# Attention in one core's two-layer model: inverse sums transposed later, low parts of the output weights pinned in order

## The chip, the cores and the metric

The program runs on one core of a Trainium2 chip. TensorE (PE) multiplies, VectorE (DVE), ScalarE (ACT) and GpSimd (POOL) do the rest, SyncE (SP) issues most of the transfers. The metric is the device time of one execution in microseconds (us): 1930.66 for the kernel before, the median of 3 runs (1925.57 to 1931.99).

## The reference

Two layers on 512 tokens of width 1024, in float32, and a last normalisation. Each layer is a feed-forward stage (added at half weight), a mixer and a second feed-forward stage; the mixer of the first layer joins gated linear attention with softmax attention of 8 heads, that of the second lets 16 heads look at the best keys only.

```
for layer in range(2):
    x = x + 0.5 * swiglu(rmsnorm(x, g[0]), ffn_w_in[layer, 0], ffn_w_out[layer, 0])
    h = rmsnorm(x, g[1])
    x = x + (even_mixer(h) if layer % 2 == 0 else odd_mixer(h))
    x = x + 0.5 * swiglu(rmsnorm(x, g[2]), ffn_w_in[layer, 1], ffn_w_out[layer, 1])
return rmsnorm(x, final_norm_g)

even_mixer: concat(gla(h), softmax(q k / 8 + F_i - F_j) v) @ even_w_out     # causal, 8 heads of 64
odd_mixer:  score = sum_h w_h relu(q_idx_h k_idx)                # 8 heads, causal
            idx = top_k(score, 128)                              # per query
            p = softmax(q_lat c[idx] / 8 + t5_bias)              # 16 heads
            (p c[idx]) @ w_uv @ odd_w_out
```

## The kernel before, in words

Activations lie with features on the 128 partitions and the 512 tokens along the free dimension, in 8 tiles of 128x512. A float32 product is made of three products of rounded parts: weights and activations are each split into a high part (`whi`, rounded by ACT) and a low part (`wlo`, the rest, subtracted by DVE), and `mm3` (L195 to L200) multiplies high with high, high with low and low with high. `Weights.split` (L76 to L89) makes the two parts of 1024 columns of a load; it is called from `at` when a product first needs them, one piece ahead. There are 3 buffers each for high and low parts and 2 for the raw loads (`wraw`).

The stages follow each other: feed-forward 0, even mixer, feed-forward 1 and 2, odd mixer, feed-forward 3. In the odd mixer the search for the best keys (`topk`, from L1137) finds 8 maxima (`m8`) and strikes them out of the scores (`acc`), 16 times for each of three blocks of queries, on DVE. It is woven with the products of the queries.

`attention` (from L639) serves both mixers. Its work is a list of units, one for each pair of heads, block of 128 queries (`b`, 0 to 3) and head of the pair, so 8 units a pair; block `b` sees 128(b+1) keys. There are 4 pairs in the even mixer and 8 in the odd one. In step `i` of the main loop: the bias of unit i+2 is added up on POOL, the scores of unit i are multiplied on PE (bank `s`) and joined with the bias on DVE, which also finds the row's extreme (L665, tiles `p` and `l`); the probabilities of unit i-4 are transposed on PE (bank `pt`, L680) and copied out, by ACT or DVE in turn (L683, L685, tiles `pts`); ACT takes the exponential of unit i (L672) and sums it. Values (`values`, L688) of block `b` are multiplied six steps after its second unit into the bank `o`.

At the end of a pair DVE inverts the 8 columns of sums and spreads them (L724, L725, tile `r`); four transposes on PE bring them to the layout of `o` (L701), ACT copies them out (L703, `rb`); two steps after the last values of the pair DVE multiplies `o` by `rb` (L708, called the normalisation here), ACT rounds the result (L712), DVE takes its low part (L715).

PSUM has 2 banks for `ps`, 3 for `s`, 2 for `pt` and 1 for `o`. PE executes in the order in which the code is written (`manual_schedule`). On the other engines a scheduler orders the instructions by program position and its own estimate of when they are ready; `keep_in_program_order` takes an instruction out of that choice. All engines work off their own order one instruction after the other, and the tracker of tiles adds the waits.

`out_units` (from L541) is the output projection: 4 loads of 2048 columns, each for two tiles of the result, 8 groups of three products for a tile. Groups 0 to 6 of the first three tiles are mixed into the last 8 steps of the attention, two groups a step; the rest follows.

Of the kernel before, what the change touches and what calls it, by code (L numbers as in the profile page):

```python
# [8 lines left out]
F32 = mybir.dt.float32  # L9
# [8 lines left out]
KT = D // 128  # L18
# [12 lines left out]
NB = S // 128  # L31
# [10 lines left out]
class Filler:  # L42


    def __init__(self):
        self.q, self.done = [], set()
# [22 lines left out]
class Weights:  # L69


    def __init__(self, b, raw, n, piece, pool_lo):
        self.b, self.raw, self.n, self.piece, self.pool_lo = b, raw, n, piece, pool_lo
        self.parts = {}

    def split(self, j):  # L76
        b, nc = self.b, self.b.nc
        c = j * self.piece
        if c >= self.n or j in self.parts:
            return  # L80
        m = min(self.piece, self.n - c)
        hi, lo = b.wtile(m)
        x = self.raw[:, c:c + m]
        nc.scalar.activation(hi, x, AF.Copy)  # L84
        if self.pool_lo:
            nc.gpsimd.tensor_tensor(lo, x, hi.bitcast(F32), op=OP.subtract)
        else:
            nc.vector.tensor_sub(lo, x, hi.bitcast(F32))  # L88
        self.parts[j] = (hi, lo)  # L89

    def at(self, c, m):
# [72 lines left out]
class Builder:  # L164
# [34 lines left out]
        mm(ps, w[0], x[1], start=False, stop=False)  # L199
        mm(ps, w[1], x[0], start=False, stop=last)  # L200

    def load_w(self, src, n, pool_lo=False, piece=1024, cuts=()):
        raw = self.wraw.tile([128, n], F32, name="wraw")
        e = [0, *cuts, n]
        for a, b in zip(e[:-1], e[1:]):
            self.nc.sync.dma_start(raw[:, a:b], src[:, a:b])
        return Weights(self, raw, n, piece, pool_lo)

    def scaled(self, i, gcol):

# [330 lines left out]
    def out_units(self, src, O, after):  # L541

        nc = self.nc
        W, P = {}, {}

        def part(d, ks):
            for k in ks:
                self.mm3(P[d], W[d // 2].at((d % 2 * KT + k) * 128, 128), O[k], k == 0, k == KT - 1)

        def begin(d, tag):  # L550
            if d % 2 == 0:
                W[d // 2] = self.load_w(src[d // 2], 2 * KT * 128)
            P[d] = self.bank(tag)

        def end(d):
            with self.tc.high_priority(offset=60):
                nc.vector.tensor_add(self.X[:, d], P[d], self.X[:, d])
                after(d)

        early = 3  # L560
        for d in range(early):
            begin(d, "ps" if d < 2 else "pt")
            for k in range(KT - 1):
                part(d, [k])
                yield 0.65
        yield "last"
        self.next_in()
        for d in range(early):
            part(d, [KT - 1])
            end(d)  # L570
        for d in range(early, KT):
            begin(d, "ps")
            part(d, range(KT))
            end(d)
# [64 lines left out]
    def attention(self, n_pairs, setup, A, head, bias, fill, act_share, ahead):  # L639

        nc = self.nc
        units = [(pair, b, hh) for pair in range(n_pairs) for b in range(NB) for hh in range(2)]
        P, T, H, steps = {}, {}, {}, []

        def add_bias(i):
            pair, b, hh = units[i]  # L650
            P[units[i]] = bias(H[2 * pair + hh], 2 * pair + hh, b)

        def scores(pair, b, hh):
            a = A[pair]
            if "l" not in a:
                a["l"] = self.at.tile([128, 16], F32, name="l", bufs=3)
            n = 128 * (b + 1)
            s = self.bank("s")
            q, kh, kl = a["qk"]
            for k in (kh, kl):  # L660
                nc.tensor.matmul(s[:, :n], q[hh][:, b * 128:b * 128 + 128], k[hh][:, :n], start=k is kh, stop=k is kl)  # L661
            t = P[pair, b, hh]
            u = 2 * b + hh
            m = a["l"][:, 8 + u:9 + u]
            nc.vector.tensor_tensor_reduce(out=t[:, :n], in0=s[:, :n], in1=t[:, :n], scale=-1.0, scalar=3.0e38,  # L665
                                           op0=OP.add, op1=OP.min, accum_out=m)

        def exps(pair, b, hh):
            l = A[pair]["l"]
            u = 2 * b + hh  # L670
            t = P[pair, b, hh][:, :128 * (b + 1)]
            nc.scalar.activation(t, t, AF.Exp, bias=l[:, 8 + u:9 + u], scale=-1.0, accum_out=l[:, u:u + 1])  # L672

        def transpose(i):
            u = units[i]
            n = 128 * (u[1] + 1)
            pt = self.bank("pt")
            t = P.pop(u)
            for k in range(0, n, 128):
                nc.tensor.transpose(pt[:, k:k + 128], t[:, k:k + 128], self.ident)  # L680
            ts = self.at.tile([128, S], F32, name="pts", bufs=5)
            if i % 4 < act_share:
                nc.scalar.activation(ts[:, :n], pt[:, :n], AF.Copy)  # L683
            else:
                nc.vector.tensor_copy(ts[:, :n], pt[:, :n])  # L685
            T[u] = ts

        def values(i, pair, b):  # L688
            a = A[pair]
            if b == 0:  # L690
                a["o"] = self.bank("o")
            for kb in range(b + 1):
                for hh in range(2):
                    v = a["V"][kb][:, a["vcol"] + hh * 64:a["vcol"] + hh * 64 + 64]
                    nc.tensor.matmul(a["o"][hh * 64:hh * 64 + 64, b * 128:b * 128 + 128], v,  # L695
                                     T[pair, b, hh][:, kb * 128:kb * 128 + 128], start=kb == 0, stop=kb == b)
            if b == NB - 2:

                rb = self.bank("pt")
                for c in range(NB):  # L700
                    nc.tensor.transpose(rb[:, c * 128:c * 128 + 128], a["r"][:, c * 128:c * 128 + 128], self.ident)  # L701
                a["rb"] = self.at.tile([128, S], F32, name="pts", bufs=5)
                nc.scalar.activation(a["rb"], rb, AF.Copy)  # L703
            if b == NB - 1:
                o = []

                def norm():
                    nc.vector.tensor_mul(a["rb"], a["o"], a["rb"])  # L708

                def high():  # L710
                    o.append(a["dst"]())
                    nc.scalar.activation(o[0][0], a["rb"], AF.Copy)  # L712

                def low():
                    nc.vector.tensor_sub(o[0][1], a["rb"], o[0][0].bitcast(F32))  # L715

                for j, f in enumerate((norm, high, low)):
                    later.setdefault(i + 2 + j, []).append(f)

        def inverse(a):  # L720

            a["r"] = self.at.tile([128, S], F32, name="pts", bufs=5)
            l = a["l"][:, :8]
            nc.vector.reciprocal(l, l)  # L724
            nc.vector.tensor_copy(a["r"].rearrange("p (u d) -> p u d", d=64), l[:, :, None].to_broadcast([128, 8, 64]))  # L725

        def prepare(i):

            pair = units[i][0]
            for h in range(2 * pair, 2 * min(pair + 2, n_pairs)):  # L730
                if h not in H and (h < 2 or i % 8 > 3):
                    H[h] = head(h)
            for p in range(pair, min(pair + 1 + ahead, n_pairs)):
                if p not in A and (p == 0 or i % 8 > 0):
                    g = setup(p)
                    next(g)
                    steps.append(g)
            if steps:
                try:
                    next(steps[0])  # L740
                except StopIteration:
                    steps.pop(0)

        n = len(units)
        later = {}
        prepare(0)
        for i in range(BIAS_LEAD):
            add_bias(i)
        for i in range(n + LAG + 3):
            if i < n:  # L750
                prepare(i)
                if i + BIAS_LEAD < n:
                    add_bias(i + BIAS_LEAD)
                scores(*units[i])
            if 0 <= i - LAG < n:
                transpose(i - LAG)
            if i < n:
                exps(*units[i])
                if i % 8 == 7:
                    later.setdefault(i + 2, []).append(lambda a=A[units[i][0]]: inverse(a))  # L760
            for f in later.pop(i, ()):
                f()
            fill(i)
            j = i - LAG - 2
            if 0 <= j < n and units[j][2] == 1:
                values(i, *units[j][:2])
        for i in sorted(later):
            for f in later[i]:
                f()
# [621 lines left out]
```

## Time and profile before

| what | value |
|---|---|
| median of 3 runs | 1930.66 us (1925.57, 1930.66, 1931.99) |
| profiled execution, its own time | 1925.84 us |
| its span, first to last instruction | 1924.0 us |
| mean granted clock of TensorE | 0.991 of 2.4 GHz |
| busy in the span | PE 1866.9 us, DVE 1467.4, ACT 907.5, POOL 217.8 |

Busy times are sums over engines that work side by side. What one instruction costs is read where it stands: in the chain of work that ended last, or in what an engine waited for. The even attention ends at about 591 us of the span, the odd one at about 1534; behind each comes the rest of its output projection.

### The profile page before, as it was taken

What the parts mean: (1) busy time and instruction counts of PE and PEld (TensorE: products, weight loads), DVE (VectorE), ACT (ScalarE), POOL (GpSimd) and SP (SyncE); (2) the same over time, 40 slices, a digit from 0 to 9 for tenths busy, and PEclk for the clock granted to TensorE, in tenths of its full rate; (3) what the DMA queues carried; (4) which work ended last, traced back from release to release, by engine and by line L of the source; (5) the groups of instructions that cost most, each with busy time, mean ns of one, the idle gap of its engine ahead of it and who ended that gap; (6) DMA issues with size and microseconds to landing.
All of it is one profiled execution on the core that took longest, in us unless ns stands there. A gap on an engine that the chain in (4) does not pass through costs nothing.

```text
span 1924.0 us, 30748 instructions
## 1 busy us (share of the span) xinstructions
PE 1866.9 (97%) x12504; PEld 1677.3 (87%) x12504; DVE 1467.4 (76%) x1929; ACT 907.5 (47%) x1275; POOL 217.8 (11%) x211
## 2 busy tenths in 40 slices
PE   6999999999999999999999999999998999999997
PEld 6989999787877999989899998987776789899996
DVE  6969677557466978859798795864898699697774
ACT  6535435334364644525554352543537565354353
POOL 0000000200161000000110000011258420000001
PEclk9999999999999999999999999999999999999998
DMA  4232322322351223332422324224256223323322
GB/s 160 84 123 92 118 99 67 120 71 94 101 157 66 88 91 107 110 110 67 153 75 90 121 81 129 77 87 142 71 153 179 75 83 102 123 89 110 110 67 77
DMA packets 60510, 198.17 MB, mean 103 GB/s; under 512 B 7880, under 2 KB 8056, under 8 KB 57296
## 3 DMA queue, kind: packets, MB, share of 16 engines
q1 hardware_dynamic: 57712, 191.65, 31.5%
q10 hardware_dynamic: 2304, 4.20, 0.8%
q8 instruction: 98, 1.61, 0.3%
q0 software_dynamic: 352, 0.36, 0.1%
q14 instruction: 44, 0.36, 0.1%
HBM read 178.03 MB, written 2.15 MB: 94 GB/s over the span
## 4 chain that ended last, share of the span: by engine, by line
PE 84%; DVE 12%; ACT 1%; DMA 1%; issue 1%; SPq 0%; DVEq 0%; ACTq 0%
PE ps L345 25%; PE pt L345 12%; PE s L200 6%; PE s L345 6%; PE s L198 6%; PE s L199 6%; PE ps L198 3%; PE ps L199 3%; PE ps L200 3%; DVE tl L223 2%; PE s L661 2%; DVE acc L1148 1%; DVE wlo L88 1%; PE o L695 1%; PE pt L680 1%
## 5 line engine op out<-in xcount | busy, mean ns | idle before, releaser
L345 PE MATMUL ps<-th,whi 128*128 128x256 f32 x1408 | 394.8, 280 | 10.0 <-ACT whi L159 10.0
L345 PE MATMUL ps<-th,wlo 128*128 128x256 f32 x1408 | 394.1, 280 | 1.1 <-DVE wlo L160 1.1
L345 PE MATMUL ps<-tl,whi 128*128 128x256 f32 x1408 | 393.4, 279 | 0.0
L84 ACT ACTIVATE whi<-wraw 128x1024 fp32r<-128x1024 f32 (+3 forms) x156 | 157.3, 1009 | 347.4 <-PE s L199 135.6
L345 PEld LDWEIGHTS ps<-th,whi 128*128 128x128 f32 x1408 | 265.5, 189 | 10.7 <-ACT whi L159 10.0
L345 PEld LDWEIGHTS ps<-th,wlo 128*128 128x128 f32 x1408 | 265.5, 189 | 1.8 <-DVE wlo L160 1.8
L345 PEld LDWEIGHTS ps<-tl,whi 128*128 128x128 f32 x1408 | 265.6, 189 | 0.6
L159 ACT ACTIVATE whi<-a 128x1024 fp32r<-128x1024 f32 x132 | 140.0, 1061 | 144.3 <-PE pt L345 43.9
L200 PE MATMUL s<-hh,wlo 128*128 128x512 f32 x528 | 205.9, 390 | 0.0
L199 PE MATMUL s<-hl,whi 128*128 128x512 f32 x528 | 205.6, 389 | 0.0
L198 PE MATMUL s<-hh,whi 128*128 128x512 f32 x528 | 205.6, 389 | 0.0
L345 PE MATMUL pt<-th,whi 128*128 128x256 f32 x704 | 197.4, 280 | 5.1 <-ACT whi L159 5.1
L88 DVE TENSOR_TENSOR wlo<-wraw,whi 128x1024 fp32r<-128x1024 f32 (+3 forms) x144 | 168.6, 1172 | 39.5 <-ACT whi L84 39.2
L345 PE MATMUL pt<-th,wlo 128*128 128x256 f32 x704 | 197.4, 280 | 0.7 <-DVE wlo L160 0.7
L345 PE MATMUL pt<-tl,whi 128*128 128x256 f32 x704 | 197.0, 280 | 0.0
L259 POOL TENSOR_TENSOR ss<-ss,sq 128x512 f32<-128x512 f32 x41 | 63.7, 1553 | 1130.8 <-ACT sq L255 1130.7
L160 DVE TENSOR_TENSOR wlo<-a,whi 128x1024 fp32r<-128x1024 f32 x132 | 160.9, 1219 | 6.1 <-ACT whi L159 6.1
L159 ACT ACTIVATE whi<-wraw 128x1024 fp32r<-128x1024 f32 x88 | 93.4, 1062 | 131.7 <-PE ps L345 51.7
L433 DVE SCALAR_TENSOR_TENSOR dn<-s,R 128x512 f32<-128x512 f32 x72 | 49.7, 690 | 122.1 <-PE s L200 122.1
L345 PEld LDWEIGHTS pt<-th,whi 128*128 128x128 f32 x704 | 133.2, 189 | 5.4 <-ACT whi L159 5.4
L345 PEld LDWEIGHTS pt<-th,wlo 128*128 128x128 f32 x704 | 133.0, 189 | 1.2 <-DVE wlo L160 1.2
L345 PEld LDWEIGHTS pt<-tl,whi 128*128 128x128 f32 x704 | 133.2, 189 | 0.0
(291 smaller groups left out, 4283.5 us busy)
## 6 DMA issues: line engine op xcount, KB each, us to landing
wraw<-in_ffn_in_dram SPq DMA_DIRECT2D x88, 512.0 KB, 4.8
a<-in_ffn_in_dram SPq DMA_DIRECT2D x88, 512.0 KB, 3.6
wraw<-in_ffn_out_dram SPq DMA_DIRECT2D x64, 512.0 KB, 3.5
wraw<-in_ffn_out_dram SPq DMA_DIRECT2D x32, 384.0 KB, 3.1
x<-x SPq DMA_DIRECT2D x62, 128.0 KB, 2.3
wraw<-in_even_fox_dram SPq DMA_DIRECT2D x4, 1024.0 KB, 4.8
wraw<-in_even_out_dram SPq DMA_DIRECT2D x4, 1024.0 KB, 5.8
wraw<-in_odd_q_dram SPq DMA_DIRECT2D x8, 512.0 KB, 3.3
```

Of the source, the lines that this page charges most:

```text
L84: nc.scalar.activation(hi, x, AF.Copy)
L88: nc.vector.tensor_sub(lo, x, hi.bitcast(F32))
L159: b.nc.scalar.activation(o[0], x, AF.Copy)
L160: b.nc.vector.tensor_sub(o[1], x, o[0].bitcast(F32))
L198: mm(ps, w[0], x[0], start=first, stop=False)
L199: mm(ps, w[0], x[1], start=False, stop=False)
L200: mm(ps, w[1], x[0], start=False, stop=last)
L223: v.tensor_sub(l, src, h.bitcast(F32))
L259: nc.gpsimd.tensor_tensor(self.ss, self.ss, sq, op=OP.add)
L345: mm(o, w[:, c], x, start=fresh and f == j == i == 0, stop=j == 3 and i == 2, skip_group_check=True)
L433: nc.vector.scalar_tensor_tensor(t, bank, 0.5, R, op0=OP.mult, op1=OP.mult)
L661: nc.tensor.matmul(s[:, :n], q[hh][:, b * 128:b * 128 + 128], k[hh][:, :n], start=k is kh, stop=k is kl)
```

## The change

The transposes of the inverse sums and their copy move from the values of block 2 to those of block 3, ahead of that block's products: two units later. And the low parts of the first load of the output weights (`d == 0`) are subtracted with `keep_in_program_order`. Lines behind L72 of the changed kernel are higher by one.

```diff
-    def __init__(self, b, raw, n, piece, pool_lo):
+    def __init__(self, b, raw, n, piece, pool_lo, pinned=False):
         self.b, self.raw, self.n, self.piece, self.pool_lo = b, raw, n, piece, pool_lo
+        self.keep = b.tc.keep_in_program_order if pinned else lambda x: x
...
-            nc.vector.tensor_sub(lo, x, hi.bitcast(F32))
+            self.keep(nc.vector.tensor_sub(lo, x, hi.bitcast(F32)))
...
-    def load_w(self, src, n, pool_lo=False, piece=1024, cuts=()):
+    def load_w(self, src, n, pool_lo=False, piece=1024, cuts=(), pinned=False):
...
-        return Weights(self, raw, n, piece, pool_lo)
+        return Weights(self, raw, n, piece, pool_lo, pinned)
...
-                W[d // 2] = self.load_w(src[d // 2], 2 * KT * 128)
+                W[d // 2] = self.load_w(src[d // 2], 2 * KT * 128, pinned=d == 0)
...
+            if b == NB - 1:
+
+                rb = self.bank("pt")
+                for c in range(NB):
+                    nc.tensor.transpose(rb[:, c * 128:c * 128 + 128], a["r"][:, c * 128:c * 128 + 128], self.ident)
+                a["rb"] = self.at.tile([128, S], F32, name="pts", bufs=5)
+                nc.scalar.activation(a["rb"], rb, AF.Copy)
             for kb in range(b + 1):
...
-            if b == NB - 2:
-
-                rb = self.bank("pt")
-                for c in range(NB):
-                    nc.tensor.transpose(rb[:, c * 128:c * 128 + 128], a["r"][:, c * 128:c * 128 + 128], self.ident)
-                a["rb"] = self.at.tile([128, S], F32, name="pts", bufs=5)
-                nc.scalar.activation(a["rb"], rb, AF.Copy)
```

The order of DVE near the end of the search for the best keys, before. `wlo` is a low part of the first output weights, MAX and MATCH_REPLACE are the search.

```order
L1146 MAX m_13709<-acc_12994 128x8
L88 TENSOR_TENSOR wlo<-wraw,whi 128x1024
L1148 MATCH_REPLACE acc_12994<-m_13709,acc_12994 128x512
L1146 MAX m_13745<-acc_12994 128x8
L1148 MATCH_REPLACE acc_12994<-m_13745,acc_12994 128x512
L1146 MAX m_13748<-acc_12994 128x8
L1148 MATCH_REPLACE acc_12994<-m_13748,acc_12994 128x512
L1069 SCALAR_TENSOR_TENSOR x<-ps,R 128x512
L1146 MAX m_13757<-acc_12994 128x8
L88 TENSOR_TENSOR wlo<-wraw,whi 128x1024
L1148 MATCH_REPLACE acc_12994<-m_13757,acc_12994 128x512
L1146 MAX m_13760<-acc_12994 128x8
```

And there in the change:

```order
L1147 MAX m_13709<-acc_12994 128x8
L1149 MATCH_REPLACE acc_12994<-m_13709,acc_12994 128x512
L1147 MAX m_13745<-acc_12994 128x8
L1149 MATCH_REPLACE acc_12994<-m_13745,acc_12994 128x512
L1147 MAX m_13748<-acc_12994 128x8
L1149 MATCH_REPLACE acc_12994<-m_13748,acc_12994 128x512
L1147 MAX m_13757<-acc_12994 128x8
L1070 SCALAR_TENSOR_TENSOR x<-ps,R 128x512
L1149 MATCH_REPLACE acc_12994<-m_13757,acc_12994 128x512
L1147 MAX m_13760<-acc_12994 128x8
```

The two low parts in this stretch are gone from it; the rest is the same work, with the scaling of one query tile a place later.

The order of DVE at the sixth step from pair to pair of the odd attention, before: `p,l<-s,p` joins scores and bias, `pts<-pt` copies transposed probabilities, `pts<-o,pts` is the normalisation.

```order
L665 ISA p,l<-s,p 128x384
L665 ISA l 128x1
L708 TENSOR_TENSOR pts<-o,pts 128x512
L665 ISA p,l<-s,p 128x512
L665 ISA l 128x1
L685 COPY pts<-pt 128x256
L665 ISA p,l<-s,p 128x512
L665 ISA l 128x1
L685 COPY pts<-pt 128x256
L665 ISA p,l<-s,p 128x128
```

There in the change:

```order
L666 ISA p,l<-s,p 128x384
L666 ISA l 128x1
L666 ISA p,l<-s,p 128x512
L666 ISA l 128x1
L686 COPY pts<-pt 128x256
L666 ISA p,l<-s,p 128x512
L666 ISA l 128x1
L686 COPY pts<-pt 128x256
L709 TENSOR_TENSOR pts<-o,pts 128x512
L725 RECIPROCAL l<-l 128x8
```

The normalisation stood ahead of the last two score units of the block and their copies, and stands behind them now.

The order of DVE at the tail of the odd attention, before, from the last two score units on:

```order
L708 TENSOR_TENSOR pts<-o,pts 128x512
L665 ISA p,l<-s,p 128x512
L665 ISA l 128x1
L685 COPY pts<-pt 128x256
L665 ISA p,l<-s,p 128x512
L665 ISA l 128x1
L685 COPY pts<-pt 128x256
L715 TENSOR_TENSOR x<-pts,x 128x512
L724 RECIPROCAL l<-l 128x8
L725 COPY pts<-l 128x512
```

And in the change:

```order
L666 ISA p,l<-s,p 128x512
L666 ISA l 128x1
L686 COPY pts<-pt 128x256
L709 TENSOR_TENSOR pts<-o,pts 128x512
L89 TENSOR_TENSOR wlo<-wraw,whi 128x1024 x2
L716 TENSOR_TENSOR x<-pts,x 128x512
L725 RECIPROCAL l<-l 128x8
L89 TENSOR_TENSOR wlo<-wraw,whi 128x1024
L726 COPY pts<-l 128x512
L686 COPY pts<-pt 128x512 x2
```

Three low parts of 1024 columns and the normalisation now stand behind the copies and ahead of the spread of the last inverse sums.

## Rows read from the trace of the kernel before

**Rows 1.** The page: shares of the chain of waits by engine.

```profile
PE 84%; DVE 12%; ACT 1%; DMA 1%; issue 1%; SPq 0%; DVEq 0%; ACTq 0%
```

**Rows 2.** The chain, end of the search: start us, us, what.

```profile
1431.78 1.12 DVE wlo L88
...
1437.80 1.19 DVE wlo L88
```

**Rows 3.** PE in order of time: start us, us, what [idle before <-releaser].

```profile
1443.22 1.44 PE L661 MATMUL s<-x 128*128 128x256 f32 x4 [4.34 <-DVE l L665]
```

**Rows 4.** PE's waits: for what, us in total, times, longest us.

```profile
PE pt L701 <- DVE pts L685: 5.2, 5, 1.6
```

**Rows 5.** Odd tail: stretch, us, then busy us of the engines and PEclk.

```profile
1519.00:1534.00 15.00, 15.00 (x103) 11.45 (x101) 4.09 (x11) 3.44 (x8) 0.00 (x0) 1.00 0.30 106
```

**Rows 6.** Stretches at the start of the odd attention.

```profile
1442.00:1444.00 2.00, 0.78 (x3) 0.78 (x4) 1.73 (x9) 0.00 (x0) 1.55 (x2) 0.50 0.38 88
...
1448.00:1449.00 1.00, 1.00 (x8) 0.49 (x6) 1.00 (x4) 0.71 (x2) 0.92 (x2) 0.64 0.92 209
```

**Rows 7.** PE in order of time, two long waits elsewhere.

```profile
975.28 0.58 PE L345 MATMUL s<-th,wlo 128*128 128x256 f32 x1 [3.17 <-DVE wlo L160]
...
1372.26 0.50 PE L199 MATMUL ps<-x,whi 128*128 128x512 f32 x1 [1.83 <-DVE x L322]
```

**Rows 8.** Stretches behind three waits of PE.

```profile
558.00:560.00 2.00, 0.92 (x10) 0.78 (x10) 1.41 (x5) 1.45 (x3) 1.68 (x4) 1.00 0.29 63
...
979.00:981.00 2.00, 2.00 (x12) 2.00 (x10) 0.93 (x2) 0.83 (x1) 0.00 (x0) 0.50 0.00 0
...
1374.00:1376.00 2.00, 2.00 (x6) 1.54 (x5) 1.47 (x3) 0.42 (x2) 0.00 (x0) 0.50 0.06 25
...
1376.00:1378.00 2.00, 2.00 (x8) 1.55 (x8) 1.56 (x5) 0.19 (x1) 0.00 (x0) 0.74 0.03 8
```

**Rows 9.** Even tail, PE and DVE in order of time.

```profile
577.43 0.40 PE L200 MATMUL ps<-x,wlo 128*128 128x512 f32 x1
...
579.12 0.68 DVE L715 TENSOR_TENSOR x<-pts,x 128x512 fp32r<-128x512 f32 x1
```

**Rows 10.** Odd tail, PE and DVE in order of time.

```profile
1519.61 0.40 PE L200 MATMUL ps<-x,wlo 128*128 128x512 f32 x1
...
1520.45 0.68 DVE L715 TENSOR_TENSOR x<-pts,x 128x512 fp32r<-128x512 f32 x1
```

**Rows 11.** DVE by line in 1450 to 1520 us: count, busy us, mean ns.

```profile
L715 DVE TENSOR_TENSOR x<-pts,x 128x512 fp32r<-128x512 f32 x6 | 7.7, 1289 | 0.0
```

**Rows 12.** Even attention, first step of pairs, DVE and PE in order of time.

```profile
558.26 0.67 DVE L708 TENSOR_TENSOR pts<-o,pts 128x512 f32<-128x512 f32 x1
...
559.08 0.44 PE L695 MATMUL o<-pts,v 128*64 128x128 f32 x4 [2.15 <-DVE l L724]
```

**Rows 13.** Odd attention, sixth step: DVE, then PE, in order of time.

```profile
1506.83 0.56 DVE L665 CUSTOM_DVE_ANT_0 p<-s,p 128x384 f32<-128x384 f32 x1 [0.26 <-PE s L661]
...
1508.61 0.69 DVE L708 TENSOR_TENSOR pts<-o,pts 128x512 f32<-128x512 f32 x1 [0.59 <-PE o L695]
...
1509.31 0.69 DVE L665 CUSTOM_DVE_ANT_0 p<-s,p 128x512 f32<-128x512 f32 x1
...
1511.20 0.28 DVE L665 CUSTOM_DVE_ANT_0 p<-s,p 128x128 f32<-128x128 f32 x1
...
1505.69 0.66 PE L701 MATMUL pt<-ident,pts 128*128 128x128 f32 x4 [0.28 <-DVE pts L685]
...
1508.42 0.74 PE L661 MATMUL s<-xgl,xgh 128*128 128x512 f32 x2
...
1509.99 0.44 PE L695 MATMUL o<-pts,v 128*64 128x128 f32 x4
```

**Rows 14.** Two periods of pairs in the odd attention: stretch, us, busy us.

```profile
1465.15:1475.80 10.65, 9.11 (x82) 6.94 (x81) 9.74 (x26) 8.63 (x26) 9.01 (x10) 1.00 0.65 161
...
1506.34:1515.59 9.25, 9.11 (x82) 6.94 (x81) 8.18 (x25) 7.18 (x23) 7.25 (x8) 1.00 0.01 4
```

## The prediction

> **What bounds the kernel now.** I read the page first: the chain of waits is 84% PE and 12% DVE [rows 1]. So work that is moved on VectorE (DVE) counts only where PE waits for it, or where it begins to make PE wait. The change touches the two attention stages and the output projections behind them, about 530 to 600 us and 1430 to 1545 us. There I read the chain, then the list of PE's waits, then both engines in order of time, with the order of the changed kernel beside them. Four places matter.
>
> First, the end of the search for the best keys. From 1431 us the chain runs on DVE, and two low parts of the first output weights (`wlo`, 1.12 and 1.19 us) lie in it [rows 2]. PE then waits 4.34 us for the first scores [rows 3]. Second, the step from one pair of heads to the next, where PE waits at the transposes of the inverse sums, 5.2 us in 5 waits over the whole trace [rows 4]. Third and fourth, the two tails, where the last transposes and values of the attention alternate with the first products of the output projection: in the odd stage PE is busy for 15.00 of 15.00 us there [rows 5], and the even stage's tail looks the same. A stall that is put in there is paid in full.
>
> **Part 1: the low parts.** Two are pinned, those of the first load. In the new order of DVE the one after them, of the second load, has moved with them: three stand at the tail of each stage that stood early.
>
> Removed, odd stage: 1.12 + 1.19 = 2.31 us of the chain. The third stood at the start of the attention. PE ran at half clock there, 1.2 GHz, from 1442 until about 1448.7 us [rows 6], after its idle spell, which is now 4.34 - 2.3, about 2.0 us. If the clock no longer falls, at most half of the 5.5 us from 1443.2 on comes back, 2.8; if it falls as before, nothing. Waits of 1.83 and 3.17 us elsewhere [rows 7] were each followed by half clock [rows 8], so I expect it to fall again, sooner and for a shorter time, and with the third low part gone from DVE I take 0.8 us (ends 0 and 2.8). Gain: 3.1 us.
>
> Removed, even stage: DVE has waits of its own behind two of the three, for POOL and for PE, and PE is dense with projections there. I take 0; the end on the good side is one low part, 1.2.
>
> Added, even tail: the third product of the projection reads the first low part. It ran at 577.43, and DVE's last copy of a score unit ended at 579.12, where the next instruction begins [rows 9]. In the new order the normalisation (0.69) and the first low part (1.15, the mean of the two in the chain) follow that copy: 579.12 + 0.69 + 1.15 = 580.95. PE stands 3.5 us. The attention's values that could fill this are queued behind the waiting product, and nothing later on PE has slack.
>
> Added, odd tail: the product ran at 1519.61, the last copy ended at 1520.45 [rows 10]. There the normalisation stood ahead of the scores; behind them it lets the copy end 0.35 us sooner, at 1520.1, since the scores now wait for PE. 1520.1 + 0.69 + 1.15 = 1521.95, against a product that would start 0.2 us sooner, at 1519.4: 2.5 us.
>
> The second pinned part is read seven groups of three products later and is hidden, the third later still. The first buffer of raw weights is held to the tail, so SP issues the third load of output weights only there; three loads for the next feed-forward stage are queued behind it, all of them used long after the attention. The third load is first split when the first products end, some 10 us after it has landed: 0. SP's moves for the attention, behind which it no longer cuts in, come a little sooner: 0.
>
> A subtraction of 512 columns took 1.29 us in the middle of the attention [rows 11] and 0.68 in the tail [rows 10]; POOL works in the one and not in the other. At the tails I use the short kind. The Trainium skill (SBUF — State Buffer, "SBUF: two separate sides") says that a VectorE instruction with two SBUF inputs and a GpSimd one that reads SBUF exclude each other, the loser waiting out the whole instruction. By that rule the even tail is dearer, by about 1.0 us as an estimate from that page, if POOL's last addition slips beside the low part, and the sum below would be 9.6 and not 8.6. POOL ends ahead of it in the trace, so I leave this out.
>
> **Part 2: the inverse sums.** Four transposes and a copy stay as they were in all 12 places, only later. PE loses its waits there. But the scheduler's order of DVE changes: the normalisation (it reads the one `o` bank, which the next pair's first values write) now stands behind two 512-wide score units and their copies in two steps of the even stage and four of the odd one where it stood ahead of them; in three odd ones it stays ahead. The trace has one normalisation that is so late, and PE stood 2.15 us behind it [rows 12].
>
> The step at 1505 to 1512 us, worked through [rows 13]: the 384-wide scores start when the copy ends, at 1506.57, not 1506.83. PE, no longer held by the transposes, issues the first 512-wide scores 0.2 us sooner; they are ready at 1508.95. DVE has no normalisation to do meanwhile and idles until then. The two units and copies took 1.9 us (1509.31 to 1511.20), so they end at 1510.85, the normalisation at 1511.5, and the next `o` starts 1.5 us behind 1509.99. In the pair after it PE has 9.11 us of work in 9.25 [rows 14], so about 0.1 is given back: 1.4 us lost.
>
> At the two like it around 1468 and 1478 us DVE is the slower engine, busy for 9.74 of a pair's 10.65 us [rows 14]; PE's new stall takes the place of an old one, and what counts is the growth of DVE's idle time: about 0.7 before the first score and, where no other work stands behind the normalisation, 0.7 after it, less 0.3 gained ahead. I take 1.1 and 0.4. In the three where the normalisation stays ahead it now waits for ACT's copy of the inverse sums, which has moved behind two 384-wide exponentials: 0.3 to 0.5 us each, 1.1 together. The odd stage loses 1.4 + 1.1 + 0.4 + 1.1 = 4.0 us. The even stage's second step costs PE about 1 us, which DVE no longer waits for POOL afterwards: 0. The last step of each stage is in the tails. Ends: all 5.2 us gained and nothing lost; or 2.15 lost in three late steps and 0.5 in three others, 8.0.
>
> **The clock at the tails.** PE now stands 3.5 and 2.5 us in them. After the 3.17 us it ran at half clock until 981 us, after the 1.83 us through 1374 to 1377, but after the 2.15 us it kept 2.4 GHz [rows 8]. I take one stretch of about 3.4 us of dense work at half clock, 1.7 us lost; ends 0 and 5.1 (one stretch twice that long and one short one).
>
> **Sum**, against the profiled execution, 1925.84 us with a span of 1924.0: -3.1 + 3.5 + 2.5 + 4.0 + 1.7 = +8.6 us, 1934.4. That execution lies at the low end of the runs (1925.57, 1930.66, 1931.99). From the middle of their range, 1928.8, and 1.9 below their median, the forecast is 1937.
>
> **Rivals.** Balanced: DVE does the same work in every pair, the late normalisation is caught up, and the clock holds: -3.1 + 6.0 = +2.9, about 1932. For it speaks that DVE is the slower engine in most odd pairs; against it the 2.15 us of the one late normalisation.
>
> Faster: the waits at the transposes were what paced the pairs and all 5.2 go, the clock holds at the start of the attention (2.3 + 2.8), and the tails cost only their stalls: -10.3 + 6.0 = -4.3, about 1924.5. It decides from the point where the normalisation runs before PE wants `o`. For it: PE had such waits in five pairs. Against: the order in which DVE now takes its work.
>
> Much slower: every late step costs the 2.15 and both tails fall to half clock: -3.1 + 6.0 + 8.0 + 5.1 = +16, about 1945. For it the 2.15 and 3.17 us rows; against it that DVE is the slower engine in most odd pairs, where a wait of PE is not the pair's length.
>
> That the change does nothing is excluded by the new order.
>
> **How the numbers follow.** About 0.3%, 5.8 us, is what a measurement can tell from no change. The forecast has 0.46, balanced 0.32, much slower 0.13, faster 0.09. A fifth of the forecast's share lies below 5.8 us, a tenth of the balanced one's above it, and a little of the faster one's falls short of the bound: slower 0.53, same 0.39, faster 0.08. The range goes from 1928, the balanced case counted from the runs' low end, to 1945, the much slower one.
>
> **What would show it.** Right: PE waits for `wlo` at the third product of both projections, by 3.5 and 2.5 us; the search ends 2.3 us sooner; PE waits 1 to 2 us for `o` in four odd steps, and not at the inverse sums' transposes; a half-clock stretch stands behind the even tail's stall. Wrong: if the waits in the tails are under 1 us, the tail terms fail; if the odd pairs are not longer than before, Part 2 fails; and if the stall in the tails is made good before the projection ends, PE had slack that I did not see.

## The result and the profile after

The changed kernel takes 1944.83 us (median of 6 runs, 1939.68 to 1946.19) against 1928.86 for the kernel before in the same runs: a ratio of 1.0086, 95% interval 1.0070 to 1.0101. It is 16 us slower, where the sum of the prediction had 8.6: the direction holds, the size is nearly double. The profiled execution has a span of 1944.4 us, 20.4 more than before's.

Where the 20.4 us lie, I read by laying both traces over each other: the same instruction of PE in both, and how much later it starts. 17.9 us are added in the two attention stages with their tails. The rest is elsewhere, where the programs are alike: PE is 3.3 us later from 34 us on, has no half-clock stretch near 975 us where before had one (-3.1), waits 1.5 more near 1350 and loses 0.8 in the last 20 us.

The shares of the chain of waits have hardly moved, against [rows 1]:

```profile
PE 83%; DVE 12%; ACT 2%; issue 1%; DMA 1%; POOL 0%; SPq 0%; DVEq 0%; ACTq 0%; POOLq 0%
```

So the chain's shares can't tell what went wrong. The list of PE's waits can (what PE waited for, us in total, times, longest us):

```profile
PE ps L201 <- DVE wlo L89: 8.2, 6, 2.5
PE o L703 <- DVE l L725: 5.9, 3, 2.0
...
PE o L703 <- DVE pts L709: 3.3, 2, 2.0
PE s L662 <- DVE l L666: 3.2, 1, 3.2
PE pt L697 <- ACT pts L684: 2.9, 3, 1.7
```

The 5.2 us at the transposes [rows 4] are gone, and 2.9 us behind ACT's copies stand in their place. The waits for `o`, the bank that the normalisation frees, are 9.2 us (two rows, five waits), where before had the one of 2.15 [rows 12]. The low parts of the output weights now make PE wait in both tails. Rows of PE (start us, us, what [idle before <-releaser]): search's end, one late step, and the two tails, against [rows 3, 9, 10]:

```profile
1449.82 1.44 PE L662 MATMUL s<-x 128*128 128x256 f32 x4 [3.22 <-DVE l L666]
...
1523.97 0.44 PE L703 MATMUL o<-pts,v 128*64 128x128 f32 x4 [1.97 <-DVE l L725]
...
585.09 0.50 PE L201 MATMUL ps<-x,wlo 128*128 128x512 f32 x1 [2.53 <-DVE wlo L89]
...
1537.47 0.50 PE L201 MATMUL ps<-x,wlo 128*128 128x512 f32 x1 [2.54 <-DVE wlo L89]
```

And the clock behind such waits (stretch, us, busy us (count) of PE, weight loads, DVE, ACT, POOL, then the granted clock, DMA share and GB/s):

```profile
586.00:588.00 2.00, 2.00 (x10) 1.33 (x9) 2.00 (x5) 0.04 (x1) 0.00 (x0) 0.50 0.43 70
1490.60:1493.60 3.00, 3.00 (x19) 2.34 (x18) 2.00 (x7) 2.21 (x7) 3.00 (x3) 0.50 0.79 177
1524.70:1527.70 3.00, 3.00 (x18) 2.34 (x18) 1.69 (x6) 1.74 (x6) 2.11 (x2) 0.50 0.03 5
1538.40:1541.40 3.00, 3.00 (x13) 2.03 (x12) 2.29 (x5) 0.49 (x1) 0.00 (x0) 0.50 0.57 172
```

PE is dense in all four and runs at 1.2 GHz; none of the four was there before.

The late step in its main rows: the sixth of the odd stage, which the prediction worked through [rows 13]. DVE, then ACT, then PE:

```profile
1518.86 0.55 DVE L666 CUSTOM_DVE_ANT_0 p<-s,p 128x384 f32<-128x384 f32 x1
...
1521.25 0.69 DVE L666 CUSTOM_DVE_ANT_0 p<-s,p 128x512 f32<-128x512 f32 x1 [1.83 <-PE s L662]
...
1522.21 0.68 DVE L666 CUSTOM_DVE_ANT_0 p<-s,p 128x512 f32<-128x512 f32 x1
...
1523.15 0.68 DVE L709 TENSOR_TENSOR pts<-o,pts 128x512 f32<-128x512 f32 x1
...
1520.20 0.58 ACT L699 ACTIVATE pts<-pt 128x512 f32<-128x512 f32 x1
...
1518.77 0.66 PE L697 MATMUL pt<-ident,pts 128*128 128x128 f32 x4
1519.35 1.09 PE L703 MATMUL o<-pts,v 128*64 128x128 f32 x16
1520.38 0.73 PE L662 MATMUL s<-xgl,xgh 128*128 128x512 f32 x2
```

The reader is to see two engines that wait for each other. DVE stands for 1.83 us until PE has the 512-wide scores, since PE has the transposes and 16 products of values ahead of them. The normalisation could have run from 1520.78, when ACT's copy ends, but in DVE's order it is behind both score units and both copies. It ends at 1523.83, and PE, whose next values want `o` from 1522.0 on, stands for 1.97 us.

### The profile page after: what moved, and what is told of

Same layout as the page of the kernel before. It is cut to its first block, busy times and chain, and to the rows that moved or that the text cites. A ratio compares the mean times of both kernels' runs of the same rounds, so it can differ in the third digit from the quotient of the medians.

```text
span 1944.4 us, 30721 instructions
## 1 busy us (share of the span) xinstructions
PE 1876.3 (96%) x12504; PEld 1685.1 (87%) x12504; DVE 1460.5 (75%) x1929; ACT 907.5 (47%) x1275; POOL 216.3 (11%) x211
## 3 DMA queue, kind: packets, MB, share of 16 engines
HBM read 178.03 MB, written 2.15 MB: 93 GB/s over the span
## 4 chain that ended last, share of the span: by engine, by line
PE 83%; DVE 12%; ACT 2%; issue 1%; DMA 1%; POOL 0%; SPq 0%; DVEq 0%; ACTq 0%; POOLq 0%
PE ps L346 25%; PE pt L346 12%; PE s L201 6%; PE s L199 6%; PE s L200 6%; PE s L346 6%; PE ps L199 3%; PE ps L201 3%; PE ps L200 3%; DVE tl L224 2%; PE s L662 2%; PE o L703 2%; DVE acc L1149 1%; DVE wlo L89 1%; PE pt L681 1%
```

## The experiments

Theory A: the loss in the attention is the late normalisation on DVE, not the moved transposes; the tails pay for the low part; half clock is added behind such stalls. Theory C, the rival: the late transposes themselves cost it (PE and DVE wait for ACT's copies in front of them). Theory B: the tails carry nearly all of it.

All times are medians; the ratio is to the kernel before, run beside them (1928.43 us for e1 to e4, 1927.25 for e5 to e8, 1928.19 for e9).

| run | us | ratio, 95% interval |
|---|---|---|
| e1_pin_only | 1932.73 | 1.0025 (1.0010 to 1.0039) |
| e2_late_rb_only | 1941.39 | 1.0063 (1.0042 to 1.0084) |
| e3_late_norm_only | 1939.56 | 1.0061 (1.0041 to 1.0082) |
| e4_norm_first | 1939.22 | 1.0060 (1.0039 to 1.0082) |
| e5_fill | 1941.17 | 1.0066 (1.0047 to 1.0086) |
| e6_best | 1925.33 | 0.9988 (0.9975 to 1.0002) |
| e7_norm_middle | 1934.67 | 1.0036 (1.0023 to 1.0050) |
| e8_two_o | 1944.64 | 1.0088 (1.0068 to 1.0108) |
| e9_late_rb_norm_middle | 1930.27 | 1.0012 (0.9996 to 1.0028) |

Stage by stage, from the traces: the time from the first score product of one pair to that of the next (the tail: from the last pair's to a fixed product behind it), less the same interval before, in us. "Start" is the end of the search and the first pair; step k is the time of pair k+1, in which `o` goes over from pair k to pair k+1.

| kernel | even steps 1, 2 | even tail | odd start | odd steps 1 to 6 | odd tail | sum |
|---|---|---|---|---|---|---|
| changed | -0.13, 2.11 | 4.09 | -2.29 | 1.31, 2.04, 1.69, 0.42, 1.01, 2.09 | 5.57 | 17.9 |
| e1 | -2.22, 0.59 | 4.72 | -1.63 | 0.50, 0.00, -0.01, -1.23, 1.20, -0.38 | 4.07 | 5.6 |
| e2 | -0.14, 2.11 | 0.42 | -0.32 | 2.09, 1.85, 2.12, 0.41, 1.02, 2.09 | 1.91 | 13.6 |
| e3 | -0.01, 3.56 | 0.33 | -0.65 | 0.22, 2.04, 1.81, 2.03, 0.99, 1.77 | 1.78 | 13.9 |
| e4 | -2.16, 1.06 | 4.75 | -2.34 | 1.24, 0.61, 4.17, 0.37, 1.01, 0.05 | 2.79 | 11.6 |
| e5 | -0.13, 3.63 | 2.61 | -1.19 | -0.47, 2.04, 1.68, 0.68, 1.01, 2.09 | 2.55 | 14.5 |
| e6 | -1.98, 0.99 | 0.91 | -1.19 | -0.39, -0.01, 0.00, -1.23, 2.62, -0.26 | 0.12 | -0.4 |
| e7 | -1.41, 0.87 | 4.21 | -1.19 | 0.44, 0.78, -0.43, -0.78, 1.02, 0.81 | 4.07 | 8.4 |
| e8 | 0.12, 4.90 | 4.15 | -1.20 | 0.20, 0.00, 4.29, 0.49, 1.01, 0.05 | 5.96 | 20.0 |
| e9 | -1.41, 0.87 | 0.65 | -0.32 | 0.81, 0.14, -0.43, -0.08, 2.79, 0.81 | -0.25 | 3.6 |

**e1, Part 1 alone.** The kernel before with `pinned=d == 0` and what it needs.

> Part 1 alone: the low parts pinned, the inverse sums transposed where they were before. The order of DVE keeps every normalisation ahead of the two 512-wide score units. Theory A (the loss of the changed kernel is the late normalisation, some 11 of 18 us in the two attention stages, the rest the tails): 2.5 us gained at the search's end, about 1.8 us stall at each tail (0.7 less than the 2.53 measured after, since the normalisation is not ahead of the low part) with or without half clock behind it: +1 to +4 us against before, 1930 to 1933. Theory B (the tails carry it, the low parts being most of the 16 us): +8 us or more, 1937 and above.

Measured +4.3 us, at the upper end. The search ends earlier by what it did in the whole change (PE waits 3.22, not 4.34 us), PE stands 2.79 us in the even tail and 2.20 in the odd one, both followed by half clock: 4.72 + 4.07. Theory B falls. A gain that nobody asked for came along: with the low parts gone from there, the scheduler puts the even stage's first normalisation early, and the wait of [rows 12] is gone (-2.22).

**e2, Part 2 alone.** The changed kernel with the pin left out:

```diff
-                W[d // 2] = self.load_w(src[d // 2], 2 * KT * 128, pinned=d == 0)
+                W[d // 2] = self.load_w(src[d // 2], 2 * KT * 128)
```

> Part 2 alone: the four transposes and the copy moved, no low part pinned. The normalisation stands behind the two 512-wide units in the even stage and in four of the odd steps. Theory A: odd steps +9 to +10 us, even step +1.7, tails 0 to 1, nothing gained at the search's end: +10 to +12 us, 1939 to 1941; PE waits about 2 us for o in three odd steps. Theory B: at most +4, 1933. This run can't tell the late normalisation from the late transposes; the next two do.

Measured +13.0 us, a little over A. Part 2 is the larger part.

**e3, the late normalisation alone.** The kernel before; the edit has nothing of the change but the place of one instruction on DVE. The scheduler then also moved some of ACT's roundings and of DVE's low parts around it:

```diff
-                    nc.vector.tensor_mul(a["rb"], a["o"], a["rb"])
+                    ins = nc.vector.tensor_mul(a["rb"], a["o"], a["rb"])
+                    if (pair in ((0, 1, 2) if n_pairs == 4 else (1, 2, 5, 6))):
+                        self.tc.keep_in_program_order(ins)
```

> The kernel before with one thing changed: DVE's normalisation is pinned behind the two 512-wide units and their copies in just the pairs in which it stands there in the changed kernel (three of the even stage, odd pairs 2, 3, 6 and 7). Transposes of the inverse sums, their copy and the low parts stay as before. Theory A (the late normalisation itself): nearly the whole price of Part 2, +8 to +12 us, 1937 to 1941, with waits of about 2 us for o. Theory C (the late transposes: PE and DVE wait for ACT's copies in front of them): 0 to +2 us, 1929 to 1931, because PE's old waits at the transposes give the time back.

Measured +11.1 us, with the early transposes of before: A's number, and 8 us and more above C's. PE in order of time in the odd stage:

```profile
1478.21 0.44 PE L695 MATMUL o<-pts,v 128*64 128x128 f32 x4 [1.97 <-DVE pts L708]
1490.66 0.44 PE L695 MATMUL o<-pts,v 128*64 128x128 f32 x4 [1.97 <-DVE pts L708]
1499.11 0.33 PE L680 MATMUL pt<-ident,p 128*128 128x128 f32 x1 [2.26 <-ACT pts L703]
...
1526.00 0.44 PE L695 MATMUL o<-pts,v 128*64 128x128 f32 x4 [1.97 <-DVE l L726]
```

The waits of 1.97 us for `o` are like those of the changed kernel. The 2.26 us for ACT has no counterpart there: about 2 us of e3's price are in step 4, behind that wait.

**e4, the whole change with the normalisation first.** The normalisation is issued with the values, and the first 512-wide score unit is queued behind it:

```diff
+            if u == 6 and pair > 0:
+                self.tc.add_manual_dep(ins.ins, A[pair - 1]["n"].ins.name, mybir.DependencyInfo(mybir.DependencyClass.NoSync, mybir.DependencyReason.DATA), reason="norm first")
```

> The whole change, with DVE's normalisation kept ahead of the 512-wide units in every pair (the first of them is queued behind it). Theory A: only the tails' stalls and the search's end are left, with 0.3 to 0.5 us in a pair for the wait of the normalisation for ACT's copy, which PE's vanished waits at the transposes (5.2 us before) pay for: +1 to +5 us against before, 1930 to 1934. Theory C: still +12 to +16, 1941 to 1945.

Measured +10.8 us: a miss for A, and on the time alone nearer to C. The table says otherwise: the late steps 2 and 6 cost 0.61 and 0.05, and step 3 alone 4.17. There the order of DVE was changed in another place too. Two low parts stand ahead of a copy for which PE waits (DVE, then PE):

```profile
1477.57 1.77 DVE L615 TENSOR_TENSOR p<-x 128x512 fp32r<-128x512 f32 x1
1479.26 1.75 DVE L718 TENSOR_TENSOR x<-pts,x 128x512 fp32r<-128x512 f32 x1
1480.93 0.68 DVE L688 COPY pts<-pt 128x512 f32<-128x512 f32 x1
...
1481.66 0.47 PE L683 MATMUL pt<-ident,p 128*128 128x128 f32 x1 [2.36 <-DVE pts L688]
```

Half clock followed. So e4 alone decides nothing, and I tried other ways.

**e5, work in the stalls.** Matmuls that nothing reads, ahead of the first product of both projections and of two of the late values:

```diff
+                if d == 0 and k == 0:
+                    z = self.bank("s")
+                    for _ in range(10):
+                        nc.tensor.matmul(z, w[0], O[k][0], start=True, stop=True)
...
+                if n_pairs == 8 and pair in (3, 6):
+                    q, kh, kl = a["qk"]
+                    z = self.bank("ps")
+                    for _ in range(5 if pair == 3 else 8):
+                        nc.tensor.matmul(z, q[0][:, :128], kh[0], start=True, stop=True)
```

> The whole change, with matmuls that nothing reads put on PE where it stands still: 10 of 512 columns ahead of the first product of both output projections, and 5 and 8 ahead of the first values of the odd stage's pairs 4 and 7 (behind the waits of 1.32 and 1.97 us for o). They give PE work in the stalls and shorten none. Theory D (each of the four new half-clock stretches is the consequence of the stall ahead of it, and costs about 1.5 us): the four stretches go, the even tail costs about 2.7 us against before in place of 4.35, the odd one 2.7 in place of 4.3, the step of pair 7 about 2.2 in place of 3.7: 1945 - 6 = 1939. Rival E (the clock falls there for another reason, or the stretches lie beside other waits): the stretches stay, 1945 or a little more, for what the matmuls take beyond the stalls.

PE's row in the even tail, and the clock in the places of three of the four stretches:

```profile
585.53 2.54 PE L553 MATMUL s<-x,whi 128*128 128x512 f32 x10
...
588.78 0.50 PE L201 MATMUL ps<-x,wlo 128*128 128x512 f32 x1 [0.25 <-DVE wlo L89]
```

```profile
589.00:591.00 2.00, 2.00 (x13) 1.31 (x13) 2.00 (x4) 0.07 (x1) 0.00 (x0) 1.00 0.16 29
1527.00:1530.00 3.00, 3.00 (x29) 2.36 (x28) 2.44 (x7) 1.58 (x8) 2.17 (x2) 1.00 0.00 0
1541.00:1544.00 3.00, 3.00 (x23) 2.24 (x22) 0.69 (x1) 0.00 (x0) 0.00 (x0) 1.00 0.97 320
```

All four are gone: they follow the stall. The even tail falls from 4.09 to 2.61, the odd one, which holds two of them, from 5.57 to 2.55: 1.5 us each, three times. The fourth, behind the late values that end step 3, cost nothing (step 4: 0.42 with it, 0.68 without): at full clock PE only waits longer for ACT (2.61 us for a copy, not 0.82). The time fell by 3.7 us (1944.83 to 1941.17) and not by 6. That the fourth cost nothing is one reason; in the profiled execution the even stage's second step also ran partly at half clock (3.63 for 2.11).

**e7, the normalisation one place earlier.** The whole change with this:

```diff
-                    nc.vector.tensor_mul(a["rb"], a["o"], a["rb"])
+                    with self.tc.high_priority(offset=40):
+                        nc.vector.tensor_mul(a["rb"], a["o"], a["rb"])
```

> The whole change with the normalisation one place earlier where it was late: behind the first of the two 512-wide units, ahead of its copy, the second unit and its copy, which took some 1.3 us together. Theory A (what PE pays is how late the normalisation ends): the waits for o fall from about 2.0 to about 0.7 us and two half-clock stretches in the pairs go: the odd steps cost 3 to 6 us in place of 10, the even one about 0.5: 1936 to 1940. Theory C (the late transposes set the price, wherever the normalisation stands): 1943 to 1945.

Measured 1934.67, better than A said. At the sixth step (DVE, then PE):

```profile
1512.43 0.69 DVE L666 CUSTOM_DVE_ANT_0 p<-s,p 128x512 f32<-128x512 f32 x1 [1.83 <-PE s L662]
...
1513.05 0.69 DVE L710 TENSOR_TENSOR pts<-o,pts 128x512 f32<-128x512 f32 x1
...
1513.88 0.44 PE L703 MATMUL o<-pts,v 128*64 128x128 f32 x4 [0.69 <-DVE pts L710]
```

The wait is 0.69 us in place of 1.97, and the six odd steps cost 1.8 us together in place of 8.6. The transposes are where the change put them.

**e8, a second bank for `o`.** The whole change, with PE's wait for the normalisation taken away in all odd steps but the last, which lies in the tail:

```diff
-                a["o"] = self.bank("o")
+                a["o"] = self.bank("ps" if n_pairs == 8 and pair in (1, 3, 5) else "o")
```

> The whole change, with the values of the odd stage's pairs 2, 4 and 6 in a bank of the tag ps, which nothing else uses before the tail; so in all odd steps but the last PE needn't wait for the normalisation of the pair before. Theory A: the waits of 1.96, 1.32 and 1.97 us for o go, and the two half-clock stretches behind them: the odd steps cost 0 to 3 us in place of 10: 1935 to 1939. Theory C: PE's waits for ACT's copies and the transposes remain and take the place of the others: 1942 to 1945.

Measured 1944.64, on the time a miss for A. The waits for `o` are gone in the odd stage and steps 2 and 6 cost 0.00 and 0.05. But the scheduler moved the two low parts ahead of the copy in step 3 as in e4 (4.29, with half clock), the even stage's second step ran partly at half clock (4.90), and the odd tail took 0.4 us more. In step 3 PE waits 0.98 us behind that copy and 1.58 at the moved transposes, for ACT, with half clock behind it. So C has a share in this one step, and e8 is no clean test of A.

**e9, Part 2 alone with the normalisation in the middle.** e2 with the lines of e7.

> Part 2 alone (no low part pinned), with the normalisation behind the first of the two 512-wide units and ahead of the rest, as in the run of the whole change with the normalisation in the middle. Theory A (the whole price of Part 2 is how late the normalisation stands): the odd steps cost 0 to 2 us, the even ones -1.4 to +0.9, the tails under 0.7: 1927 to 1930, against 1941 for Part 2 with the late normalisation. Theory C (a price of 5 us and more stays with the late transposes): 1933 or more.

Measured +2.1 us, against +13.0 for e2, which differs by the place of the normalisation and what the scheduler does with it. The transposes are as late in both. That settles the main part for A: moving the normalisation takes away 10.9 us by the medians, 10.0 in the table, of which 1.3 are the even stage's first step, whose normalisation was late in the kernel before too. What stays with the late transposes is small and not well known: +2.1 us, from -1 to +5 by the interval. The odd steps, at 4.0 us in the table, missed A's 0 to 2; 2.79 of them are step 5, where the clock fell to 0.50 behind waits of 0.58, 0.35 and 0.36 us.

**e6, the gains without the losses.** The kernel before with the odd stage's first low part on POOL, once its last bias is added up, and the even stage's first normalisation kept early:

```diff
+            W[0] = self.load_w(src[0], 2 * KT * 128, pinned=True)
+            W[0].pool_lo = True
+            W[0].split(0)
+            W[0].pool_lo = False
...
+            if i == 8 * n_pairs - 3:
+                next(out)
...
+                    with self.tc.high_priority(offset=60 if n_pairs == 4 and pair == 0 else 0):
```

> A version meant to keep the gains and none of the losses. Odd stage: the first low part of the output weights is subtracted on POOL, pinned to a place three steps before the last scores, where POOL has nothing left to do (2.48 us there against 1.15 on DVE); the second and third stand in the tail. Even stage: low parts as before, and the normalisation of the first pair ahead of the 512-wide units (which took the 2.15 us wait away in the run with the pin alone). Transposes of the inverse sums as before. Theory A: -1.1 to -1.5 us at the search's end, up to -1.3 more behind it, -1.6 in the even stage, no stall in the tails: -2.5 to -4.3 us, 1924 to 1926. Rival: POOL's low part is late or slows DVE down, and a stall of about 1 us with half clock behind it at the odd tail eats the gain: 1927 to 1929.

Measured 1925.33: in the range expected, but the gain is 1.9 us where 2.5 to 4.3 were expected, and the interval reaches past 1. POOL is done in time, and no product of the odd tail waits:

```profile
1513.88 2.37 POOL L87 TENSOR_TENSOR wlo<-wraw,whi 128x1024 fp32r<-128x1024 f32 x1
```

The odd tail costs 0.12 us there. Step 5 costs 2.62: half clock follows a wait of 1.35 us for ACT. The median is the lowest of all kernels here; that it beats the kernel before is likely and not shown.

## Why the prediction was right in direction and wrong in size

The steps in the order of the sum, forecast first, then what the traces show.

- Search's end and odd start, -3.1: -2.29. Two low parts of 2.31 us went from the chain, but PE's wait fell by 1.12 only. The low part of the first keys, which ran 0.94 us before, took 1.48 (1447.48, line 615), with POOL adding up biases all the while, and the instruction ahead of it (1446.85, line 1152) 0.72 in place of 0.41. That is 0.85 us of the 1.19 that are missing; the rest stays open. The clock did fall again, as forecast.
- Even tail 3.5 and odd tail 2.5: stalls of 2.53 and 2.54. The odd one is as forecast, the even one 1.0 too high. Before, DVE waited there for POOL's biases, ahead of the last two score units:

```profile
576.62 0.69 DVE L665 CUSTOM_DVE_ANT_0 p<-s,p 128x512 f32<-128x512 f32 x1 [0.25 <-POOL p L972]
...
578.16 0.69 DVE L665 CUSTOM_DVE_ANT_0 p<-s,p 128x512 f32<-128x512 f32 x1 [0.51 <-POOL p L972]
```

In the changed kernel PE comes later, the biases are ready, and DVE no longer waits for them there.
- **Odd pairs, 4.0: 8.6** (the six steps of the table). This is the step that failed. I had taken 1.4, 1.1 and 0.4 for the three late steps; they cost 2.09, 2.04 and 1.69. For the two around 1468 and 1478 I argued that DVE was the slower engine, so that a wait of PE was not the pair's length. But busy time over a pair (9.74 of 10.65 [rows 14]) doesn't tell that: in the late steps DVE itself stands, 1.78, 2.01 and 1.83 us (the last at 1521.25), because the scores come from the PE that it holds up. For the sixth step I had PE issue the 512-wide scores 0.2 us sooner; it issued them 7.62 us behind the pair's first score, 7.56 before, since earlier in the pair it now waits 0.47 us for ACT (0.11 before, for DVE). I left out 0.14 us from PE's scores to DVE and 0.14 from the normalisation's end (1523.83) to PE, and no part of the stall was given back. The three steps with the early normalisation cost 1.31, 0.42 and 1.01, 2.7 in place of 1.1: PE now waits for ACT at the moved transposes, 2.9 us in three waits.
- **Even second step, 0: 2.0** (2.11 less 0.13). It was to be paid back by a wait of DVE for POOL; PE waited 1.97 us there, and nothing gave it back within the step. Some of it came back in the tail, as the rows above show.
- **The clock, 1.7: 4.5**, three stretches of 1.5 us (e5). One was forecast. Of the pairs I had expected none, since the single 2.15 us wait before kept 2.4 GHz [rows 8]. That was one case.

Together 17.9 against 8.6. The medians say 16.0. The rival called much slower had the price of each late step (2.15), the clock's (5.1) and the time (1945) nearly right; I gave it 0.13 for an argument from busy shares, which was the mistake. What I called a sign of being wrong did not show: no tail wait is under 1 us, the pairs are longer, the stalls in the tails are not made good. Of the signs of being right two failed: PE waits for `o` in three odd steps and not in four, and it still waits at the transposes, now for ACT.

## What to carry to other kernels

Before work is moved later on one engine, look at the order in which a scheduler will then serve the engine that frees a single buffer: one instruction that stood behind two score units, and not behind one, cost about 10 us over the two stages (e2 against e9). A busy share, however high, doesn't show that an engine sets the pace in a loop where two engines wait for each other; the idle time just ahead of the instruction in question does. And a stall of about 2 us inside dense matmuls can cost more than its length: three of the stalls here cost 1.5 us more each by the clock. That is a risk to be priced and not a fixed term, as the next section shows.

## What the runs showed of the hardware that I had not expected

Waits of the same length need not have the same effect on the clock. In e3 the wait of 1.97 us that ended at 1478.21 was followed by half clock, that of 1.97 us at 1490.66 was not:

```profile
1479.00:1481.00 2.00, 2.00 (x13) 1.67 (x13) 1.84 (x6) 1.45 (x5) 1.93 (x2) 0.50 0.61 132
1491.00:1493.00 2.00, 2.00 (x21) 1.63 (x20) 1.68 (x6) 1.07 (x3) 2.00 (x2) 1.00 0.70 157
```

Six us ahead of the first, PE had stood for 1.44 us; between the two it had no wait worth a row. And the first late normalisation of the even stage, 1.96 us in the changed kernel, in e5 and in e8, was followed by half clock in e5 and e8 only. All six stalls of 2.2 to 2.8 us for the first low part in the changed kernel, e1 and e7 were followed by it, but that of 2.10 us in e4's odd tail was not. Nor is 2.2 us a bound: in the changed kernel a wait of 2.45 us outside the attention kept the full clock.

```profile
983.40 0.38 PE L346 MATMUL s<-th,wlo 128*128 128x256 f32 x1 [2.45 <-DVE wlo L161]
```

```profile
983.00:985.00 2.00, 1.60 (x13) 1.60 (x14) 2.00 (x4) 1.01 (x2) 1.37 (x1) 1.00 0.00 0
985.00:987.00 2.00, 2.00 (x19) 2.00 (x18) 2.00 (x3) 1.51 (x2) 0.17 (x1) 1.00 0.00 0
```

In all eleven traces, 17 waits of PE lie between 2.2 and 2.8 us; half clock followed 12 of them.

Half clock cost nothing where PE had waits to come: step 4, 0.42 us in the changed kernel and 0.68 in e5.

A subtraction of 512 columns on DVE with both inputs in SBUF took 0.68 us in the tails, where POOL is idle, and 1.75 in e4 with POOL at work. The Trainium skill (SBUF — State Buffer, "SBUF: two separate sides") says that such an instruction and a GpSimd one that reads SBUF exclude each other; the two durations agree with it.
